# Low parts of split weights formed by accumulating transfers: four split tiles, three raw buffers

## The chip, the cores and the metric

The program runs on one core of one Trainium2 chip. The metric is the device time of one execution in microseconds (us); less is better. A core has five engines that run side by side, each through its own list of instructions in a fixed order: TensorE (PE, with its weight loads shown apart as PEld), VectorE (DVE), ScalarE (ACT), GpSimd (POOL) and SyncE (SP). They meet through semaphores alone. Transfers are issued from an engine's list and carried out by 16 DMA engines that all the issuing engines share.

## The reference

The reference is a two-layer encoder that is applied to two sequences, a prompt of 256 positions and a sample of 512, with 1024 features each. Every layer is modulated by a conditioning vector `c`: layer 0 mixes positions with a two-directional mLSTM of 4 heads, layer 1 with attention in a sliding window, and both end in a gated feed-forward network with a convolution over three positions. Cut to what matters:

```python
def trunk(x, c, ...):
    for l in range(DEPTH):                                   # DEPTH = 2
        mod = jax.nn.silu(c) @ adaln_w[l] + adaln_b[l]
        sh1, sc1, g1, sh2, sc2, g2 = split(mod, 6)
        h = rmsnorm(x, norm_g[l, 0]) * (1 + sc1) + sh1
        y = mlstm_mixer(h, ...) if l % 2 == 0 else swa_mixer(h, ...)
        x = x + g1 * y
        h = rmsnorm(x, norm_g[l, 1]) * (1 + sc2) + sh2
        x = x + g2 * conv_ffn(h, ffn_w_up[l], ffn_conv_w[l], ffn_conv_b[l], ffn_w_down[l])
    return rmsnorm(x, final_g)

def conv_ffn(h, w_up, conv_w, conv_b, w_down):
    u = conv(h @ w_up, conv_w) + conv_b                      # 2 * 2816 channels, width 3
    return (silu(u[..., :D_FF]) * u[..., D_FF:]) @ w_down
```

All data are float32, and the result must be accurate to nearly that.

## The kernel before

The 768 positions of both sequences are the columns of every activation, the 1024 features lie on 128 partitions in 8 groups. A matrix product in TensorE's fast rounded format (`R`, float32r) is too coarse alone, so both factors are **split**: a high part is the value rounded to that format, a low part is what the rounding left. Three matmuls, high by high, high by low and low by high, add up in PSUM to nearly the full product.

Weights come in units of 128 x 2048 values, and each is handled in two halves of 128 x 1024 (512 KB). `load` (L234) takes a half from device memory with one transfer from SP's queue into a tile named `raw`; there are **five** buffers of that name. `split` (L237) makes two tiles, `whi` and `wlo`, of which there are **three** buffers each: ACT writes `whi` by a copy that rounds (L222), then DVE writes `wlo` as the raw tile less `whi` (L223). There are 247 such splits. The rows of the conditioning matrix `adaln_w` also go through `raw` tiles, either multiplied by TensorE (`adaln`, L351) or by DVE (`adaln_v`, L412); each of these two generators fetches one row ahead of the one it uses. The small tiles `sb` (L384, L442) take a `raw` buffer too.

The stages, in order: the start (normalisation, first rows of `adaln_w`, gates), the four mLSTM heads with rows of `adaln_w` worked in between, the output gate, the output projection (`out_proj`, L509), the feed-forward network of layer 0 (`ffn`, L1117), then attention (`swa`), projection and feed-forward network of layer 1.

A feed-forward network takes 11 steps `p`, and a step is two calls of `pair` (L1045) and one of `down` (L1180). A `pair` loads two halves, `ra` and `rb`, adds and subtracts their quarters in place on POOL (L1053, L1055, L1056, L1079) and splits three tiles: `wa` from `ra` as it came, `wc` from `ra` after the additions, `wb` from `rb` after them (the sums of a scheme that takes 7 products of quarters where 8 would be needed). A fourth operand, `s1`, has half the size and its own tiles. Between the products ACT copies an accumulator from one PSUM bank to another (L1086, L1093), and the next product adds to the copy. `down` splits two halves (here D0 and D1). So a step has 8 splits and 6 loads. The gated product of the convolved rows is taken on POOL (L1165).

The order of instructions on each engine is not written by hand: a scheduler with a timing model of its own orders each engine's list, and a tile's buffer is given out again when the last reader of its former content is done. The lists are then fixed.

Of the kernel before, what the change touches and what calls it, by code (L numbers as in the profile page):

```python
# [10 lines left out]
F32 = mybir.dt.float32  # L11
R = mybir.dt.float32r
AF = mybir.ActivationFunctionType
ALU = mybir.AluOpType

P = 128
# [121 lines left out]
class Net:  # L138
# [88 lines left out]


    def raw(self, src):
        t = self.stg.tile([P, 1024], F32, tag="raw", name=self.nm("raw"), bufs=5)  # L230
        self.nc.sync.dma_start(t, src)
        return t

    def load(self, u, h):  # L234
        return self.raw(self.io["w"][u, :, h * 1024 : (h + 1) * 1024])

    def split(self, src):  # L237
        hi = self.stg.tile([P, 1024], R, tag="whi", name=self.nm("whi"), bufs=3)
        lo = self.stg.tile([P, 1024], R, tag="wlo", name=self.nm("wlo"), bufs=3)
        self.fp_copy_split(hi, lo, src)  # L240
        return hi, lo

    def halves(self, u):
        for h in range(2):
            yield h, self.split(self.load(u, h))

    def step(self, gen, n=1):
        for _ in range(n):
# [102 lines left out]
    def adaln(self, l, th, first=False):  # L351
        nc = self.nc
        hold = None

        def fetch(i):
            nonlocal hold
            k, h = divmod(i, 2)
            c0 = th * 2048 + h * 1024
            src = self.io["adaln_w"][l, k * P : (k + 1) * P, c0 : c0 + 1024]
            if k < 2 or not first:  # L360
                return self.raw(src)
            z = (i - 4) % 3
            if z == 0:
                hold = self.slab([P, 3, 1024])
            nc.sync.dma_start(hold[:, z], src)
            return hold[:, z]

        if not first:
            part = fetch(0)
            yield  # L370
        ps = self.ps()
        for i in range(2 * KC):
            k, h = divmod(i, 2)
            cur = fetch(i) if first else part
            if not first and i < 2 * KC - 1:
                part = fetch(i + 1)
            for g in range(2):
                r0 = 32 * (2 * h + g)
                self.mm(
                    ps[r0 : r0 + 32, :], self.silc[:, k, :], cur[:, g * 512 : (g + 1) * 512], k == 0, k == KC - 1  # L380
                )
            if i < 2 * KC - 1 and (h or not first):
                yield
        sb = self.stg.tile([P, 2, 256], F32, tag="raw", name=self.nm("sb"), bufs=5)  # L384
        sb = [sb[:, z] for z in range(2)]
        nc.vector.tensor_copy(sb[0], ps[:, :256])
        nc.scalar.copy(sb[1], ps[:, 256:])
        pt = self.ps()
        for b in range(4):
            nc.tensor.transpose(  # L390
                pt[:, b * P : (b + 1) * P], sb[b // 2][:, (b % 2) * P : (b % 2 + 1) * P], self.ident
            )
        src = pt.rearrange("p (b g s) -> p g b s", b=4, g=4)[:, :, :, 0:2]
        dst = self.mod[l][:, th * 16 : (th + 1) * 16, :].rearrange("p (g b) s -> p g b s", g=4)
        ab = self.cst(AB + 48 * l + 16 * th, 16).rearrange("p (g b) -> p g b", g=4)
        for s in range(2):
            nc.vector.tensor_tensor(dst[:, :, :, s], src[:, :, :, s], ab, ALU.add)
        i = {0: 0, 2: 1}.get(th)
        if i is not None:
            c0 = 8 if i == 0 else 32  # L400
            for s in range(2):
                nc.vector.scalar_tensor_tensor(
                    self.gain[l][i][:, :, s],
                    self.mod[l][:, c0 : c0 + 8, s],
                    1.0,
                    self.cst(NG + (2 * l + i) * 8, 8),
                    ALU.add,
                    ALU.mult,
                )
        yield  # L410

    def adaln_v(self, l, pool):  # L412

        nc = self.nc
        stt = nc.vector.scalar_tensor_tensor
        rows = [(grp, k) for grp in range(6) for k in range(KC)]
        fetch = lambda grp, k: self.raw(
            self.io["adaln_w"][l, k * P : (k + 1) * P, grp * 1024 : (grp + 1) * 1024]
        )
        raw = fetch(*rows[0])  # L420
        yield
        for grp, k in rows:
            if k == 0:
                acc = pool.tile([P, 2, 1024], F32, tag="ada", name=self.nm("ada"), bufs=1)
            row = raw
            if (grp, k) != rows[-1]:
                raw = fetch(*rows[grp * KC + k + 1])
            for s in range(2):
                w = self.silc[:, k, s : s + 1]
                if k == 0:  # L430
                    nc.vector.tensor_scalar(acc[:, s], row, w, None, ALU.mult)
                else:
                    stt(acc[:, s], row, w, acc[:, s], ALU.mult, ALU.add)
            if k < KC - 1:
                yield
                continue
            ps = self.ps()
            for s in range(2):
                for b in range(2):
                    r0 = 32 * (2 * s + b)  # L440
                    self.mm(ps[r0 : r0 + 32, :], self.ones[:, :32], acc[:, s, b * 512 : (b + 1) * 512], True, True)
            sb = self.stg.tile([P, 2, 256], F32, tag="raw", name=self.nm("sb"), bufs=5)  # L442
            sb = [sb[:, z] for z in range(2)]
            nc.vector.tensor_copy(sb[0], ps[:, :256])
            nc.scalar.copy(sb[1], ps[:, 256:])
            pt = self.ps()
            for t in range(4):
                nc.tensor.transpose(
                    pt[:, t * P : (t + 1) * P], sb[t // 2][:, (t % 2) * P : (t % 2 + 1) * P], self.ident
                )  # L450
            src = pt.rearrange("p (t g s) -> p g t s", t=4, g=4)[:, :, :, 0]
            ab = self.cst(AB + 48 * l + 8 * grp, 8).rearrange("p (b t) -> p b t", b=2)
            dst = self.mod[l][:, grp * 8 : (grp + 1) * 8, :].rearrange("p (b t) s -> p b t s", b=2)
            for s in range(2):
                nc.vector.tensor_tensor(dst[:, :, :, s], src[:, 2 * s : 2 * s + 2], ab, ALU.add)
            i = {1: 0, 4: 1}.get(grp)
            if i is not None:
                for s in range(2):
                    stt(
                        self.gain[l][i][:, :, s], self.mod[l][:, grp * 8 : (grp + 1) * 8, s], 1.0,  # L460
                        self.cst(NG + (2 * l + i) * 8, 8), ALU.add, ALU.mult,
                    )
            yield
# [45 lines left out]
    def out_proj(self, u0, act, xt, l, apply):  # L509


        def tiles():
            kept = []
            for u in range(4):
                for h, w in self.halves(u0 + u):
                    kept.append(w)
                    yield 0, 2 * u + h, w
            for c in (5, 6, 7):
                yield 1, c, kept[c]
            yield 1, 4, self.split(self.load(u0 + 2, 0))  # L520
            for u in range(2):
                for h, w in self.halves(u0 + u):
                    yield 1, 2 * u + h, w

        norms = [Norm(self, xt, half, apply) for half in HALVES]
        for i, (z, c, w) in enumerate(tiles()):
            c0, c1, _ = HALVES[z]
            o = self.ps()[:, : c1 - c0]
            self.product(o, w, act, c0, c1)
            self.tick(4.2)  # L530
            for p0, p1, q in pieces(c0, c1):
                self.resid(xt, o[:, p0 - c0 : p1 - c0], l, 16, c, (p0, p1, q))
            norms[z].square(c)
            if i % KC == KC - 1:
                self.start(HALVES[z], norms[z].stages())
# [13 lines left out]
    def mlstm(self, pool, gw, xt):  # L549
        nc, io = self.nc, self.io  # L550
# [57 lines left out]

        hsT = [self.slab([P, 4, T]) for _ in range(2)]
        for h in range(4):  # L610

            mb = self.slab([P, 4, T])
            for d in range(2):
# [10 lines left out]
            for i in range(2):  # L624
# [3 lines left out]
                t = self.slab([P, 2, 2, T], R)  # L628
# [30 lines left out]
            for q, (s0, s1) in enumerate(SEQS):  # L659
                n = (s1 - s0) // P  # L660
                for j in range(n):
# [7 lines left out]
                    w = (n + 1) * P  # L669
# [13 lines left out]
                    if q == 0:  # L683
                        t = [pool.tile([P, 640], R, tag="PT", name=self.nm("PT"), bufs=8) for _ in range(2)]
# [360 lines left out]
    def pair(self, pool, u, bank, rows, early=False, spare=False, pool_adds=True):  # L1045


        nc = self.nc
        r1, r2 = rows
        ra, rb = (self.load(u, h) for h in range(2))  # L1050
        q = [t[:, 512 * i : 512 * (i + 1)] for t in (ra, rb) for i in range(2)]
        tt = (nc.gpsimd if pool_adds else nc.vector).tensor_tensor
        tt(q[2], q[2], q[3], ALU.add)  # L1053
        wa = self.split(ra)
        tt(q[0], q[2], q[0], ALU.subtract)  # L1055
        tt(q[1], q[1], q[0], ALU.subtract)  # L1056
        if spare:
# [339 lines left out]
```

## Time and profile before

| What | Value |
|---|---|
| device time, median of 3 runs | 1947.95 us (1947.2 to 1950.5) |
| the profiled execution, device time | 1955.06 us |
| its span, first to last instruction | 1953.2 us |
| granted TensorE clock, mean over it | 0.979 |
| ACT copies to `whi` | 247, mean 1047 ns |
| DVE subtractions to `wlo` | 247, mean 1339 ns |
| loads of weights into `raw` by SP | 202, 512 KB each, 3.7 us to landing in the median |
| loads of `adaln_w` into `raw` | 84, 512 KB each, 4.3 us |
| transfers issued by POOL | none |

A row of the grouped views names the line, the engine, the operation, what is written and read, and how often; then the busy time in us and the mean length in ns, and behind the second bar the time that the engine stood idle before these instructions, with what ended it. In a timeline, a row has start, length, engine, line and operation, and in brackets the idle time before it and what released it. The lists of waits give the total in us, how often, and the longest. The 1.9 us between the span and the device time lie around the program's instructions.

### The profile page before, as it was taken

Reading aid. Unit: us, or ns where it says so; the run is one execution under the profiler, and the core shown is the slowest. Engines: PE = TensorE matmul, PEld = TensorE weight load, DVE = VectorE, ACT = ScalarE, POOL = GpSimd, SP = SyncE. Lnnn points to the kernel's source line nnn. Section 1 sums busy time; section 2 is a strip of 40 time slices with the busy share of each in tenths; the row PEclk is TensorE's granted clock in tenths of the full one; section 3 lists DMA queues with packets and bytes.
Section 4 is the critical chain, followed back from the end, with each engine's and each line's share of the span. In section 5 each row is a group of like instructions: output and inputs, shape, how many; then the busy total and the mean of one; then the engine's idle time right before and its main releaser. Section 6 shows DMA issues by size and latency. Waiting matters only on the chain. (4 is left out here: it accounts for less than half of the span.)

```text
span 1953.2 us, 28783 instructions
## 1 busy us (share of the span) xinstructions
PE 1851.3 (95%) x11122; PEld 1673.9 (86%) x11122; DVE 1390.8 (71%) x2261; ACT 895.8 (46%) x1785; POOL 555.1 (28%) x448
## 2 busy tenths in 40 slices
PE   6799999999979999999999999999799999999997
PEld 3686887888978999999999998779789999999997
DVE  4756675684577777777777765775877777777776
ACT  3343433343446444444444555774554444444442
POOL 4203011032213333333331311342123333333323
PEclk8899999999989999999999999999899999999998
DMA  9335445455212222222222221122212222222211
GB/s 341 100 100 188 150 155 198 150 157 169 76 44 76 65 66 65 65 65 65 65 66 87 98 89 49 40 85 76 65 56 65 72 69 66 72 68 65 65 33 66
DMA packets 63381, 181.32 MB, mean 93 GB/s; under 512 B 6071, under 2 KB 23735, under 8 KB 63244
## 3 DMA queue, kind: packets, MB, share of 16 engines
q1 hardware_dynamic: 63244, 179.49, 28.7%
q8 instruction: 87, 1.43, 0.3%
q14 instruction: 50, 0.41, 0.1%
HBM read 173.03 MB, written 6.43 MB: 92 GB/s over the span
## 5 line engine op out<-in xcount | busy, mean ns | idle before, releaser
L222 ACT CAST whi<-raw 128x1024 fp32r<-128x1024 f32 x247 | 258.5, 1047 | 414.0 <-PE pa L216 202.8
L223 DVE TENSOR_TENSOR wlo<-raw,whi 128x1024 fp32r<-128x1024 f32 x247 | 330.5, 1339 | 104.1 <-ACT whi L222 103.5
L216 PE MATMUL pa<-slab,whi 128*128 128x256 f32 (+1 forms) x1472 | 349.1, 335 | 3.7 <-DVE slab L507 2.6
L216 PEld LDWEIGHTS pa<-slab,whi 128*128 128x128 f32 x1472 | 253.4, 191 | 35.3 <-DVE slab L507 9.2
L507 DVE SCALAR_TENSOR_TENSOR slab<-pa,mod,slab 128x256 f32<-128x256 f32 (+1 forms) x368 | 206.9, 591 | 59.2 <-PE pa L216 59.1
L216 PE MATMUL pa<-slab,wlo 128*128 128x256 f32 (+1 forms) x736 | 234.6, 332 | 0.0
L216 PE MATMUL ps<-zh,whi 128*128 128x256 f32 (+2 forms) x688 | 230.1, 338 | 4.6 <-ACT zh L222 2.7
L216 PE MATMUL ps<-zh,wlo 128*128 128x256 f32 (+2 forms) x688 | 229.3, 337 | 2.8 <-DVE wlo L223 2.8
L216 PE MATMUL ps<-zl,whi 128*128 128x256 f32 (+2 forms) x688 | 231.0, 338 | 0.9 <-DVE zl L477 0.7
L1040 PE MATMUL ps<-zh,whi 128*128 128x384 f32 x504 | 173.7, 345 | 20.9 <-ACT ps L1093 18.2
L1041 PE MATMUL ps<-zl,whi 128*128 128x384 f32 x504 | 171.8, 341 | 4.1 <-DVE zl L223 4.1
L1042 PE MATMUL ps<-zh,wlo 128*128 128x384 f32 x504 | 171.5, 340 | 0.0
L216 PEld LDWEIGHTS pa<-slab,wlo 128*128 128x128 f32 x736 | 140.1, 191 | 12.3
L216 PEld LDWEIGHTS ps<-zh,whi 128*128 128x128 f32 x688 | 132.8, 194 | 20.2 <-ACT zh L222 3.5
L1053 POOL TENSOR_TENSOR raw<-raw 128x512 f32<-128x512 f32 x38 | 69.0, 1815 | 284.3 <-DMA raw<-in_w_dram 132.6
L216 PEld LDWEIGHTS ps<-zh,wlo 128*128 128x128 f32 x688 | 133.4, 194 | 14.1 <-DVE wlo L223 3.4
L216 PEld LDWEIGHTS ps<-zl,whi 128*128 128x128 f32 x688 | 133.4, 194 | 12.3 <-issue 1.7
L1130 DVE SCALAR_TENSOR_TENSOR slab<-slab,cstt,slab 128x771 f32<-128x771 f32 x88 | 131.5, 1496 | 1.4
L1165 POOL TENSOR_TENSOR slab<-slab 128x772 f32<-128x772 f32 x44 | 89.5, 2035 | 139.6 <-DVE slab L1130 124.8
L1055 POOL TENSOR_TENSOR raw<-raw,raw 128x512 f32<-128x512 f32 x38 | 49.1, 1291 | 266.5 <-DVE wlo L223 245.8
L1129 DVE SCALAR_TENSOR_TENSOR slab<-slab,cstt,slab 128x771 f32<-128x771 f32 x88 | 103.0, 1172 | 29.8 <-ACT slab L1127 29.8
L1040 PEld LDWEIGHTS ps<-zh,whi 128*128 128x128 f32 x504 | 96.2, 191 | 29.9 <-ACT ps L1093 24.0
(261 smaller groups left out, 4220.1 us busy)
## 6 DMA issues: line engine op xcount, KB each, us to landing
raw<-in_w_dram SPq DMA_DIRECT2D x202, 512.0 KB, 3.7
raw<-in_adaln_w_dram SPq DMA_DIRECT2D x84, 512.0 KB, 4.3
slab<-in_x_dram SPq DMA_DIRECT2D x12, 512.0 KB, 9.1
slab<-in_adaln_w_dram SPq DMA_DIRECT2D x12, 512.0 KB, 10.2
slab<-mrows SPq DMA_DIRECT2D x8, 384.0 KB, 4.8
xs<-slab SPq DMA_DIRECT2D x6, 512.0 KB, 2.9
bt<-brow SPq DMA_DIRECT2D x16, 192.0 KB, 3.2
slab<-xs SPq DMA_DIRECT2D x6, 512.0 KB, 9.3
```

The costliest lines, as they stand in the source:

```text
L216: self.nc.tensor.matmul(out, lhsT, rhs, start=start, stop=stop)
L222: nc.scalar.copy(hi, src)
L223: nc.vector.tensor_tensor(lo, src, hi.bitcast(F32), ALU.subtract)
L507: self.nc.vector.scalar_tensor_tensor(x, o, self.mod[l][:, gc + c, q : q + 1], x, ALU.mult, ALU.add)
L1040: mm(o, wh[:, k], hi[k], start=start and k == 0, stop=False, skip_group_check=True)
L1041: mm(o, wh[:, k], lo[k], start=False, stop=False, skip_group_check=True)
L1042: mm(o, wl[:, k], hi[k], start=False, stop=k == 3, skip_group_check=True)
L1053: tt(q[2], q[2], q[3], ALU.add)
L1055: tt(q[0], q[2], q[0], ALU.subtract)
L1129: stt(y[:, 1:], u[:, :-1], w(0), y[:, 1:], ALU.mult, ALU.add)
L1130: stt(y[:, :-1], u[:, 1:], w(2), y[:, :-1], ALU.mult, ALU.add)
L1165: nc.gpsimd.tensor_tensor(y, y, yrow[:, j], ALU.mult)
```

## The change

Where the flag `adds` is set, the low part is no longer a subtraction on DVE. ACT writes the rounded raw tile to `whi` as before, then a second time with its sign turned to `wlo`; then a transfer issued by POOL adds the unrounded weights to `wlo`, so that it holds raw less high. The transfer's source is the weight in device memory where the raw tile holds it unchanged (`origin` is given), else the raw tile itself. The flag is set from the second mLSTM head on and stays set. There are 4 buffers each of `whi` and `wlo` in place of 3, and 3 of `raw` in place of 5.

```diff
     def raw(self, src):
-        t = self.stg.tile([P, 1024], F32, tag="raw", name=self.nm("raw"), bufs=5)
+        t = self.stg.tile([P, 1024], F32, tag="raw", name=self.nm("raw"), bufs=3)
         self.nc.sync.dma_start(t, src)
         return t
 
     def load(self, u, h):
-        return self.raw(self.io["w"][u, :, h * 1024 : (h + 1) * 1024])
-
-    def split(self, src):
-        hi = self.stg.tile([P, 1024], R, tag="whi", name=self.nm("whi"), bufs=3)
-        lo = self.stg.tile([P, 1024], R, tag="wlo", name=self.nm("wlo"), bufs=3)
-        self.fp_copy_split(hi, lo, src)
+        return self.raw(self.weights(u, h))
+
+    def split(self, src, origin=None):
+        nc = self.nc
+        hi = self.stg.tile([P, 1024], R, tag="whi", name=self.nm("whi"), bufs=4)
+        lo = self.stg.tile([P, 1024], R, tag="wlo", name=self.nm("wlo"), bufs=4)
+        if self.adds:
+            nc.scalar.copy(hi, src)
+            nc.scalar.activation(lo, src, AF.Copy, scale=-1.0)
+            nc.gpsimd.dma_start(lo, src if origin is None else origin, accum_op=ALU.add)
+        else:
+            self.fp_copy_split(hi, lo, src)
         return hi, lo
+
+    adds = False
+
+    def weights(self, u, h):
+        return self.io["w"][u, :, h * 1024 : (h + 1) * 1024]
 
     def halves(self, u):
         for h in range(2):
-            yield h, self.split(self.load(u, h))
+            yield h, self.split(self.load(u, h), self.weights(u, h))
...
-        sb = self.stg.tile([P, 2, 256], F32, tag="raw", name=self.nm("sb"), bufs=5)
+        sb = self.stg.tile([P, 2, 256], F32, tag="raw", name=self.nm("sb"), bufs=3)
...
-            yield 1, 4, self.split(self.load(u0 + 2, 0))
+            yield 1, 4, self.split(self.load(u0 + 2, 0), self.weights(u0 + 2, 0))
...
         for h in range(4):
+            self.adds = h > 0
...
-        wa = self.split(ra)
+        wa = self.split(ra, self.weights(u, 0))
```

In the changed program 240 of the 247 splits go this way, 152 with the source in device memory and 88 with the raw tile; 7, all of the first head and the gates, stay as they were.

More of the change, by code (lines that the diff above doesn't have):

```diff
@@ L441, in adaln_v @@
                     self.mm(ps[r0 : r0 + 32, :], self.ones[:, :32], acc[:, s, b * 512 : (b + 1) * 512], True, True)
-            sb = self.stg.tile([P, 2, 256], F32, tag="raw", name=self.nm("sb"), bufs=5)
+            sb = self.stg.tile([P, 2, 256], F32, tag="raw", name=self.nm("sb"), bufs=3)
             sb = [sb[:, z] for z in range(2)]
```

## The prediction

> **What bounds the kernel now.** I read the page's busy shares first, then the waits of PE, then one step of a feed-forward network (from one `whi` copy of ACT to the same copy a step later) as a window.
>
> ```profile
> PE 1851.3 (95%) x11122; PEld 1673.9 (86%) x11122; DVE 1390.8 (71%) x2261; ACT 895.8 (46%) x1785; POOL 555.1 (28%) x448
> L222 ACT CAST whi<-raw 128x1024 fp32r<-128x1024 f32 x247 | 258.5, 1047 | 414.0 <-PE pa L216 202.8
> L223 DVE TENSOR_TENSOR wlo<-raw,whi 128x1024 fp32r<-128x1024 f32 x247 | 330.5, 1339 | 104.1 <-ACT whi L222 103.5
> 1656.69:1704.28 47.59, 46.80 (x266) 44.06 (x265) 36.42 (x40) 21.84 (x35) 16.89 (x10) 1.00 0.22 68
> PE ps L1040 <- ACT ps L1093: 18.4, 19, 3.2
> PE ps L216 <- DVE wlo L223: 2.8, 3, 1.7
> ```
>
> PE is busy 95% of the span, and in the step 46.80 of 47.59 us (the columns are window, length, then PE, PEld, DVE, ACT, POOL, granted clock, DMA share, GB/s). So PE's own work sets the time, and a step has 0.79 us to win. DVE stands at 36.42 us of 47.59: it is not the bound. The last row is the one that this change aims at, the wait for a low part: 2.8 us in the whole execution. The row above it is the largest wait of PE in the list, 18.4 us behind an ACT copy.
>
> **What is removed.** 240 subtractions of 1339 ns, 321 us of DVE's 1390.8. In the steps this lies beside PE's work and is worth nothing by itself. It is on the path only where DVE runs without a gap while PE waits for it, at the normalisation between `out_proj` and `ffn`:
>
> ```profile
> 554.46 1.22 DVE L223 TENSOR_TENSOR wlo<-raw,whi 128x1024 fp32r<-128x1024 f32 x1
> 559.89 1.22 DVE L223 TENSOR_TENSOR wlo<-raw,whi 128x1024 fp32r<-128x1024 f32 x1
> 562.69 0.69 PE L1041 MATMUL ps<-zl,s1h 128*128 128x384 f32 x1 [3.03 <-DVE zl L223]
> 558.66 0.44 PE L1040 MATMUL ps<-zh,s1h 128*128 128x384 f32 x1 [1.81 <-ACT zh L222]
> ```
>
> Two of them, 2.4 us, end before PE goes on at 562.69. But ACT makes one more pass there, and PE waits for ACT too (last row): I take 1.0 us of it back. 1.4 us a layer, **-3 us** for two layers; bounds -5 and +2.
>
> **What is added.** ACT gets 240 further passes. Their shape is that of the `whi` copy, so 1047 ns each, 251 us, which brings ACT from 46% to 59%. The transfers have no row here: nothing was issued by POOL. I build the time L from the end of ACT's second pass to a usable `wlo` out of the load's rows in two hundred microseconds of steps:
>
> ```profile
> q1 hardware_dynamic: 3731, 13.58, 21.9%
> L231 SPq DMA_DIRECT2D raw<-in_w_dram x26: 327/328/328, 1600.2 to 1798.6; - x26
> DMA to landing us min/median/max: 3.5/3.8/4.7
> L1079 POOL TENSOR_TENSOR raw<-raw,raw x8: 2004/2016/2026, 1620.7 to 1784.6; 128x512 f32<-128x512 f32 x8
> ```
>
> A load takes 3.8 us to land, and 21.9% of 200 us for 26 loads is 1.68 us of all 16 DMA engines each. The accumulating transfer moves the same bytes, but reads the old `wlo` as well. Issue on POOL: between 0.33 us (SP's issue) and 2.0 us (POOL's longest operation in a step); I take 1.2, halfway, since software work on POOL resembles the second row more than the first. Landing: between 3.5 us (the second read hidden) and twice 4.7 us (one after the other); I take 3.8 + 1.68 = 5.5, a load with a second read behind it. So L = 6.7 us, bounds 3.8 and 11.4. Where the DVE subtraction took 1.3 us, the low part comes some 6.5 us later (with the second pass of ACT).
>
> The Trainium skill, DMA: Bandwidth & Descriptors, section on the anatomy of a DMA on the SWDGE path, gives 2.0 us plus the bytes at 436 GB/s for a transfer issued by POOL, and Collectives: The Full Stack, section on the bandwidth ceiling, says that an add in a transfer costs a second read and no more; by both, L is an estimated 2.0 + 2 x 1.2 = 4.4 us, the steps' term below would be nothing, and the sum 1960 us. No run here shows either so far.
>
> **Is there cover for L?** In the instruction order of the changed program I looked, in a step in the middle of a network, for the tile with the least time between its buffer becoming free and its first use. It is the `wa` of the next step's first pair. Its buffer comes free with the last matmul of the second pair's `wc`, and between that and the third matmul of `wa`, the first that reads the low part, PE has 34 matmuls of `down` (512 and 256 columns by turns), 12 of 384 columns, and 2 with the high part:
>
> ```profile
> 1655.08 0.34 PE L1040 MATMUL ps<-bq,whi 128*128 128x384 f32 x1
> 1656.67 2.03 PE L216 MATMUL pa<-slab,whi 128*128 128x512 f32 x8
> 1658.54 0.40 PE L216 MATMUL pa<-slab,wlo 128*128 128x512 f32 x1
> 1681.00 0.40 PE L216 MATMUL pa<-slab,whi 128*128 128x256 f32 x2
> 1681.35 0.40 PE L216 MATMUL pa<-slab,whi 128*128 128x256 f32 x2
> ```
>
> From start to start, 9 of 384 columns take 1.59 us (0.177 each), 8 of 512 take 1.87 (0.234), 3 of 256 take 0.35 (0.117; one more lies between the last two rows). 17 x 0.234 + 17 x 0.117 + 14 x 0.177 = 8.4 us. ACT's two passes take 2.1, and for two handovers between engines I take 0.4: **5.9 us** are left for L. For `wc`, `wb` and D0 it is some 71 matmuls, 12.5 us, so 10.0 for L. The least cover meets L = 6.7, so PE waits 0.8 us a step. There are 10 such steps a network, 20 in all: **+16 us**; bounds 0 (L at most 5.9) and 20 x 5.5 = 110. Every step pays again, because the buffer's release is PE's own matmul and moves with it.
>
> POOL's list is one queue, and the transfer of D1, issued just ahead of that of `wa`, stands behind the addition that waits for the next `rb` to land; that load stands behind the release of a raw tile by the transfer of `wb`. Behind a late POOL transfer wait the quarter additions (L1053, L1055, L1056), so ACT's next `whi`, so the bank copies L1086 and L1093 in ACT's list, so PE. From the release of that buffer of `wb` to D1's first matmul with the low part PE has some 156 matmuls, 27.3 us; in them lie two passes of ACT (2.1), L, issue and landing of two loads (4.5), the addition (2.0) and L again: covered up to L = 9.3, so I add nothing for it.
>
> **Three raw buffers.** At the start four rows of `adaln_w` were loaded at once; now the fourth waits for the first to be used and stands in SP's list behind 11 other loads, and the ten rows from it on follow it in PE's list:
>
> ```profile
> 28.03 1.04 ACT L222 CAST whi<-raw 128x1024 fp32r<-128x1024 f32 x1 [5.00 <-DMA raw<-in_wg_dram]
> 28.85 0.71 PE L216 MATMUL pa<-kct,nr 128*128 128x128 f32 x4
> 33.19 1.05 PE L216 MATMUL ps<-slab,silc 128*32 128x512 f32 x4 [0.26 <-DMA slab<-in_adaln_w_dram]
> 36.14 15.36 POOL L491 TENSOR_SCALAR slab<-slab,gain,mod 128x256 f32<-128x256 f32 x16 [7.34 <-DVE gain L402]
> 51.47 6.73 POOL L106 TENSOR_TENSOR nt<-nt,nt 128x256 f32<-128x256 f32 x5
> 58.26 2.72 PE L216 MATMUL pa<-inv,nt 128*128 128x2 f32 x12 [5.92 <-POOL nt L106]
> ```
>
> The fourth row takes the place in SP's list of the load that landed at 28.0. Then PE has ten rows of 1.05 us from 29.2, and the last three after them: 42.9 where the last row ended at 34.2, 8.6 later. POOL's 16 modulations end at 60.2 and not at 51.5; but the new order puts three of POOL's five additions (1.35 us each) ahead of them, so PE's matmul that stood until 58.2 comes at 62.9: **+5 us**, bounds 3 and 8.6.
>
> In the heads the two fetchers of `adaln_w` hold one raw buffer each, which leaves one for the weights and the `sb` tiles:
>
> ```profile
> L216 PE MATMUL ps<-raw,silc x128: 592/593/617, 125.6 to 386.0; 128*32 128x512 f32 x128
> L433 DVE SCALAR_TENSOR_TENSOR ada<-raw,silc,ada x72: 1266/1279/2623, 111.6 to 441.2; 128x1024 f32<-128x1024 f32 x72
> L231 SPq DMA_DIRECT2D raw<-in_adaln_w_dram x69: 327/328/917, 107.8 to 424.7; - x69
> DMA to landing us min/median/max: 3.5/4.2/7.2
> 180.03 39.31 SPq L231 DMA_DIRECT2D raw<-in_adaln_w_dram x10
> ```
>
> A row holds a buffer for 4.2 us of landing and 2.5 of use on DVE: three buffers can pass one each 2.2 us, and the last row shows a demand of one each 3.9. So they suffice on average, but nothing is ahead any more. The 32 rows that PE uses (128 records, four to a row) stand in PE's fixed list, and a late one stops it. I take 0.3 us for each, **+10 us**; bounds 0 and a third of a landing each, 45.
>
> The other stages pass: `out_proj` uses a half in 4.2 us of PE, so a buffer has three times that, 12.5, for 2.1 + 6.7; the gate and attention stages are slower still.
>
> **The sum.** 1955.06 + 16 + 5 + 10 - 3 = 1983 us of device time for the profiled execution. That one stood 7.1 us over the median of the runs, so the forecast is **1976 us**, 1.4% slower.
>
> **The rivals.** 0.2%, 3.9 us, is about what a measurement of this kernel can tell from no change.
>
> *Faster by the fourth tile.* ACT's list stops at a `whi` copy whose buffer PE still reads, and the bank copy behind it is late:
>
> ```profile
> ACT whi L222 <- PE pa L216: 202.8, 39, 7.8
> 1682.14 1.05 ACT L222 CAST whi<-raw 128x1024 fp32r<-128x1024 f32 x1 [7.31 <-PE pa L216]
> 1683.10 0.47 ACT L1093 COPY ps<-ps 128x384 f32<-128x384 f32 x1
> ```
>
> That is PE's 18.4 us. With a fourth buffer ACT would not stop there; with L below 5.9 nothing is paid in the steps, and if the heads hide their rows: 1955 - 18 - 5 + 5 - 7 = 1930 us. Against it: ACT now makes two passes ahead of a bank copy, so that 1.05 us becomes 2.1 where it is ahead. It decides below L = 5.9.
>
> *Heavy.* L = 11.4, reads one after the other, over the cover of `wa` by 5.5 us a step and over that of the others by 1.4: 1955 + 110 + 28 + 15 - 7 = 2101. For it: POOL does in software what SP's row shows at 0.33. Against it: the engines are 22% busy, so there is room to overlap.
>
> *It changes nothing.* DVE is not the bound, and cost and gain cancel within 3.9 us: 1948.
>
> **How the numbers follow.** Forecast 0.48, heavy 0.20, faster 0.22, nothing 0.10. The forecast's own range, with L from 5.9 to 9 and the heads and the start at their bounds, is 1953 to 2035. Leaving out the lower third of the faster case and most of the heavy one, the range is 1934 to 2060. Slower 0.48 + 0.20 = 0.68, same 0.10, faster 0.22.
>
> **What would show it.** The transfers' landing time in the issues of POOL: 5.5 us, its issue 1.2. In the waits of PE: a new one for the transfer at L1042 in place of L1093, 0.8 us a step, steps of 48.4 us where they were 47.6; waits of `ps` for rows of `adaln_w` between 100 and 400 us; the last row of the start near 43 us. DVE near 1070 us, ACT near 1147, the engines' DMA share in the steps above twice 0.22. The forecast is wrong if the transfer lands before 4.7 us, or if POOL's issue costs several microseconds and the additions behind it come to set the step.

## The result and the profile after

| | before | after |
|---|---|---|
| device time, median | 1948.7 us (1947.2 to 1950.5) | 2198.1 us (2196.0 to 2200.9) |
| ratio, 95% interval | | 1.128 (1.126 to 1.130) |
| span of the profiled execution | 1953.2 us | 2197.2 us |

The kernel became 12.8% slower. The direction was predicted, the size (1976 us, at most 2060) was not. First the page of the changed kernel: busy times, ACT's second pass, the two kinds of DMA queue (packets, MB, share of 16 engines), and the issues with their median time to landing.

```profile
PE 1917.6 (87%) x11122; PEld 1726.7 (79%) x11122; DVE 1092.9 (50%) x2021; ACT 1111.0 (51%) x2025; POOL 703.1 (32%) x688
L245 ACT ACTIVATE wlo<-raw 128x1024 fp32r<-128x1024 f32 x240 | 254.0, 1058 | 0.0
L246 POOL DMA_DIRECT2D wlo<-in_w_dram x152 | 134.3, 884 | 765.7 <-ACT wlo L245 266.5
q0 software_dynamic: 34560, 125.84, 31.5%
raw<-in_w_dram SPq DMA_DIRECT2D x202, 512.0 KB, 5.4
wlo<-in_w_dram POOLq DMA_DIRECT2D x152, 512.0 KB, 7.9
wlo<-raw POOLq DMA_DIRECT2D x88, 512.0 KB, 5.0
```

PE fell from 95% busy to 87%, and no other engine took its place: the highest share is still PE's. So PE waits. In the median a transfer lands 7.9 us after the start of its issue when its source is device memory and 5.0 us when it is the raw tile; POOL's issue, 0.88 us, lies inside that time. The loads, 3.7 us before, now take 5.4.

Where the time went is read from the same stretches of both kernels: from the start to the first sigmoid of the output gate, from there to the first residual addition of `out_proj`, and in each feed-forward network from its first convolution to that of its eleventh step. First the kernel before, then the changed one (window, length, then PE, PEld, DVE, ACT, POOL, granted clock, DMA share, GB/s):

```profile
0.00:396.80 396.80, 357.44 (x2252) 290.81 (x2253) 247.73 (x424) 146.17 (x364) 69.94 (x70) 0.96 0.51 172
396.80:478.60 81.80, 77.87 (x470) 67.39 (x470) 49.23 (x72) 31.17 (x66) 30.03 (x24) 1.00 0.49 157
584.70:1037.00 452.30, 442.44 (x2489) 417.29 (x2488) 348.17 (x383) 212.29 (x333) 160.39 (x93) 1.00 0.22 67
1425.60:1878.60 453.00, 442.53 (x2488) 417.12 (x2487) 348.59 (x383) 212.21 (x332) 160.57 (x93) 1.00 0.22 67
```

```profile
0.00:472.20 472.20, 380.17 (x2281) 306.25 (x2282) 228.15 (x409) 167.11 (x391) 82.00 (x90) 0.91 0.56 167
472.20:570.70 98.50, 79.55 (x441) 68.26 (x440) 35.36 (x56) 39.54 (x70) 31.50 (x34) 0.90 0.65 170
677.70:1200.60 522.90, 465.38 (x2503) 437.13 (x2502) 250.97 (x307) 282.71 (x411) 215.16 (x173) 0.95 0.61 133
1608.10:2128.90 520.80, 464.30 (x2502) 437.35 (x2501) 249.65 (x307) 282.16 (x412) 215.91 (x173) 0.95 0.61 134
```

The lengths differ by 75.4 us (start and heads), 16.7 (gate), 70.6 and 67.8 (networks): 230.5 of the 244.0 us. Of the rest, attention takes 15 (from its first product to the first residual addition behind it, 237.2 to 252.1 us) and the stretch from there to the second network 7 (101.1 to 108.1); some others give a little back. In the first network PE's busy time rose by 22.9 us for the same products and its idle time, length less busy, from 9.9 to 57.5. The step of a network, the mean of the last eight in each, went from 47.6 to 55.6 us.

PE's waits in the whole execution (total, times, longest) name what it waited for:

```profile
PE ps L1056 <- DMA wlo<-in_w_dram: 71.3, 18, 5.7
PE ps L216 <- DMA wlo<-in_w_dram: 39.7, 14, 6.9
PE ps L1054 <- ACT nt L1121: 31.6, 15, 2.9
PE ps L216 <- ACT whi L244: 25.5, 11, 8.5
PE ps L216 <- DMA raw<-in_adaln_w_dram: 13.8, 6, 3.9
```

The first row is `wa`'s low part in the networks, the second the low parts of heads, gate and projections. The third, an ACT copy of an accumulator in the networks, belongs to the first: in ACT's list the copy stands behind work that waits for the same late load. In the second network these two rows are 37.3 and 16.7 us of PE's 56.5 idle. The chain of waits shows how one step gets there (start, length, what):

```profile
1855.97 8.17 DMA raw<-in_w_dram
1864.30 1.26 POOL raw L1067
1865.56 3.38 issue
1868.96 0.88 POOL wlo L246
1869.84 1.39 issue
1871.24 8.17 DMA wlo<-in_w_dram
1879.46 0.69 PE ps L1056
```

The load of `rb` for the next pair lands 8.2 us after its issue; POOL adds the quarters; then ACT makes four passes, a half-size copy and two short ones (the pieces called issue), POOL issues D1's transfer and `wa`'s, and `wa`'s takes 8.2 us. PE stood for 5.4 us of it. Why the load left so late is in the waits of SP's queue in the middle of the second network (1700 to 2100 us):

```profile
SPq L231 <- DMA wlo<-raw: 286.6, 28, 19.2
```

SP's list of loads stands behind the landing of the transfers that read a raw tile: with three raw tiles, the next pair's `ra` takes the tile of `wb`, and `rb` is behind `ra` in the list. In this step `wb`'s transfer landed at 1855.50, and the two loads left at 1855.55 and 1855.97. Such waits alone do no harm: with transfers that copy and don't add (below), SP waits as long, 207.5 us in 300 us, and the networks lose nothing. What counts is how much still follows the load.

### The profile page after: what moved, and what is told of

It reads as the page before. It is cut to its first block, busy times and chain, and to the rows that moved or that the text cites. A ratio compares the mean times of both kernels' runs of the same rounds, so it can differ in the third digit from the quotient of the medians.

```text
span 2197.2 us, 29235 instructions
## 1 busy us (share of the span) xinstructions
PE 1917.6 (87%) x11122; PEld 1726.7 (79%) x11122; DVE 1092.9 (50%) x2021; ACT 1111.0 (51%) x2025; POOL 703.1 (32%) x688
## 3 DMA queue, kind: packets, MB, share of 16 engines
q0 software_dynamic: 34560, 125.84, 31.5%
## 5 line engine op out<-in xcount | busy, mean ns | idle before, releaser
L244 ACT CAST whi<-raw 128x1024 fp32r<-128x1024 f32 x240 | 251.5, 1048 | 280.6 <-DMA raw<-in_w_dram 93.0
L246 POOL DMA_DIRECT2D wlo<-in_w_dram x152 | 134.3, 884 | 765.7 <-ACT wlo L245 266.5
L216 PE MATMUL pa<-slab,whi 128*128 128x256 f32 (+1 forms) x1472 | 359.8, 343 | 2.7 <-DVE slab L520 2.3
L216 PEld LDWEIGHTS pa<-slab,whi 128*128 128x128 f32 x1472 | 265.9, 200 | 29.6 <-DVE slab L520 3.3
L245 ACT ACTIVATE wlo<-raw 128x1024 fp32r<-128x1024 f32 x240 | 254.0, 1058 | 0.0
L1056 PE MATMUL ps<-yh,wlo 128*128 128x384 f32 x336 | 123.5, 368 | 71.3 <-DMA wlo<-in_w_dram 71.3
L1143 DVE SCALAR_TENSOR_TENSOR slab<-slab,cstt,slab 128x771 f32<-128x771 f32 x88 | 128.0, 1454 | 114.0 <-ACT slab L1141 114.0
L216 PEld LDWEIGHTS pa<-slab,wlo 128*128 128x128 f32 x736 | 147.2, 200 | 18.6 <-DMA wlo<-in_w_dram 5.3
L446 DVE SCALAR_TENSOR_TENSOR ada<-raw,silc,ada 128x1024 f32<-128x1024 f32 x84 | 111.0, 1360 | 58.3 <-DMA raw<-in_adaln_w_dram 58.3
L246 POOL DMA_DIRECT2D wlo<-raw x88 | 77.1, 876 | 183.3 <-issue 111.7
```

The costliest lines, as they stand in the source:

```text
L216: self.nc.tensor.matmul(out, lhsT, rhs, start=start, stop=stop)
L244: nc.scalar.copy(hi, src)
L245: nc.scalar.activation(lo, src, AF.Copy, scale=-1.0)
L246: nc.gpsimd.dma_start(lo, src if origin is None else origin, accum_op=ALU.add)
L1056: mm(o, wl[:, k], hi[k], start=False, stop=k == 3, skip_group_check=True)
L1143: stt(y[:, 1:], u[:, :-1], w(0), y[:, 1:], ALU.mult, ALU.add)
```

## The experiments

The table gives the median of the runs, the ratio to the kernel before (1949 to 1951 us beside each of them) with its interval, and from one profiled execution the start with the heads, the gate, and the step, as defined above.

| kernel | us | ratio | start, heads | gate | step |
|---|---|---|---|---|---|
| before | | | 396.8 | 81.8 | 47.6 |
| changed | 2198 | 1.128 (1.126 to 1.130) | 472.2 | 98.5 | 55.6 |
| buffers alone | 1957 | 1.003 (1.002 to 1.005) | 419.5 | 84.0 | 46.7 |
| adds, old buffers | 2223 | 1.138 (1.136 to 1.141) | 439.7 | 84.4 | 57.7 |
| device source only | 2100 | 1.076 (1.074 to 1.079) | 471.2 | 98.8 | 49.7 |
| raw source only | 1988 | 1.019 (1.017 to 1.021) | 416.4 | 85.5 | 47.9 |
| `wb` by DVE | 2094 | 1.073 (1.067 to 1.080) | 468.6 | 99.9 | 49.6 |
| `wa` by DVE | 2107 | 1.079 (1.076 to 1.083) | 468.7 | 96.9 | 50.1 |
| D0, D1 by DVE | 2086 | 1.069 (1.061 to 1.076) | 473.5 | 98.3 | 49.2 |
| second pass alone | 2020 | 1.035 (1.030 to 1.041) | 441.5 | 91.9 | 47.1 |
| heads by DVE | 2142 | 1.098 (1.095 to 1.101) | 419.5 | 83.9 | 56.1 |
| copy, not add | 1988 | one run | 441.8 | 92.5 | 46.6 |
| one set of 11 buffers | 1948 | 0.998 (0.997 to 1.000) | 392.7 | 83.3 | 47.3 |
| 4 raw, 4 high, 3 low | 1937 | 0.993 (0.991 to 0.994) | 407.3 | 80.7 | 47.2 |

### The parts of the change alone

Buffers alone:

```diff
-            self.adds = h > 0
+            self.adds = False
```

> The changed kernel with every low part by DVE's subtraction again, and the new buffers (3 raw, 4 and 4 split). In the changed kernel the start and the heads took 75 us more, the gate 17, the two feed-forward networks 138. Theory A (three raw buffers become too few only because a transfer that reads a raw tile, or lands late, holds it): steps at 47.6 us, no half-clock stretches in them, start and heads at 400 to 420 us, time 1950 to 1975. Theory B (three raw buffers alone starve the heads, the transfers the networks): start and heads near 470 us, time 2020 to 2045. Theory C (the fourth split tile frees ACT): a gain of up to 18 us in the networks, time 1930 to 1950.

Theory A gave the heads and the time, and C the sign in the networks: 46.7 us a step for 47.6. The three raw tiles cost 25 us in heads and gate, the fourth split tiles gave most of it back. ACT's wait for a `whi` buffer that this product of PE releases went from 202.8 us to 39.5 (waits of this kernel):

```profile
ACT whi L222 <- PE pa L216: 39.5, 21, 5.3
```

The transfers with the old buffers:

```diff
-tag="raw", ..., bufs=3    tag="whi", ..., bufs=4    tag="wlo", ..., bufs=4
+tag="raw", ..., bufs=5    tag="whi", ..., bufs=3    tag="wlo", ..., bufs=3
```

> The 240 accumulating transfers with the old buffers (5 raw, 3 and 3 split). Theory A (the loop that sets a step runs through the raw buffers: transfer of wb has landed, then the next pair's load, the addition on POOL, ACT's passes, the transfer of wa): with five raw buffers the loads start earlier, steps at 48 to 51 us instead of 56, time 2000 to 2080. Theory B (the prediction's: the landing of the transfer against the least cover between a split buffer's release and its next use): with three split tiles each cover is some 48 matmuls, 8.4 us, shorter, so steps of 60 us and more, time above 2280.

Neither hit: 57.7 us a step, nearer to B. Five raw tiles did not rescue the steps; that the three split tiles took away cover of their own is the likely reason, for PE now waits for the low parts of D0 and D1 and of the pairs' raw-source tiles as well:

```profile
PE pa L216 <- DMA wlo<-in_w_dram: 56.6, 18, 4.5
PE ps L1056 <- DMA wlo<-raw: 23.9, 23, 2.0
```

So raw tiles were not the whole cause, and theory A in that form fell. Five raw and four split tiles together were not tried.

Then the transfers by source, with the new buffers:

```diff
-        if self.adds:
+        if self.adds and origin is not None:      # device source only
+        if self.adds and origin is None:          # raw source only
```

> Only the 152 splits whose source lies in device memory go by transfer (wa, D0, D1, heads, gate, projections); wc and wb by DVE's subtraction, so no transfer holds a raw tile. New buffers. Theory A (raw tiles held by the transfers of wc and wb delay the loads): steps at 48 to 51 us, time 2030 to 2080, with start, heads and gate still 80 us too long. Theory B (the landing of wa's own transfer, some 8 us, is short of its cover of 5.9): PE keeps waiting for wa each step, steps of 50 to 54 us, time 2080 to 2150.

> The opposite: only the 88 splits whose source is the raw tile (wc and wb of every pair) go by transfer, all others by DVE's subtraction. New buffers. Theory A (raw tiles held by these transfers): steps at 51 to 55 us, start and heads as in the run with the buffers alone, time 2040 to 2110. Theory B (wa's landing): steps at 47.6 to 48.5, time within 20 us of the run with the buffers alone.

The first does not part the theories (49.7 us lies in A's range, the time in B's); the second is B's, with 31 us over the buffers alone where B allowed 20. Against the 46.7 us of the buffers alone the two add 3.0 and 1.2 us a step, but together, in the changed kernel, 8.9. That they do more than their sum is what a path in series would do that hides under PE's own 46.7 us until it is longer. A low part takes longer than DVE's by landing + ACT's pass - subtraction: 7.8 + 1.06 - 1.34 = 7.5 us from device memory, 5.2 + 1.06 - 1.34 = 4.9 from a raw tile (landings of these two kernels; the issue is inside them, so that the 8.5 and 5.8 of the next expectations count it twice). They then leave 49.7 - 7.5 = 42.2 and 47.9 - 4.9 = 43.0 us for the rest of the path, and 42.6 + 7.5 + 4.9 = 55.0 stands against the changed kernel's 55.6.

That the sum comes so near is in part luck. In the second kernel PE waits little for a transfer and mostly for an ACT copy behind the late load (second network), so its path has another end:

```profile
PE ps L1054 <- ACT ps L1107: 10.5, 9, 2.6
PE ps L1056 <- DMA wlo<-raw: 2.0, 3, 1.1
```

And the late load of `rb`, which the path holds, lands in 4.8 and 5.5 us in these two kernels but in 7.8 in the changed one (medians of the first pairs in the second network).

### Is it one path in series?

Each link alone given back to DVE:

```diff
-    wb = self.split(rb)                                # or wa, or D0 and D1
+    wb = self.split(rb, dve=True)
```

> The changed kernel, but wb (44 of the 240) by DVE's subtraction. Steps were 56 us in the changed kernel, 46.7 with no transfers, 50 with those from device memory alone, 48 with those from raw tiles alone. Theory A (one loop in series: wb's transfer has landed, load, addition, ACT, wa's transfer, PE, wb's copies; its rest is some 41.5 us, a transfer from device memory adds 8.5, one from a raw tile 5.8): the loop loses up to 5.8, less if wc's transfer, 1.9 us ahead, holds the other raw tile: steps of 50 to 53 us, time 2080 to 2140. Theory B (every transfer costs its share of busy DMA engines: 9.3 us for 8 a step): two fewer give 2.3, steps of 53.7, time 2150.

> The changed kernel, but wa (44 of the 240) by DVE's subtraction. Theory A (the loop): it loses the 8.5 us of wa's transfer, unless that of D1, issued 2.3 us ahead of it on POOL, takes its place: steps of 48 to 51 us, time 2030 to 2090. Theory B (share of busy DMA engines): steps of 53.7, time 2150, as with wb.

> The changed kernel, but D0 and D1 (44 of the 240) by DVE's subtraction. Theory A (the loop): the loop keeps wa's and wb's transfers, and loses ACT's second pass and POOL's issue for D1 ahead of wa (about 2.3 us) and D0's transfer beside the late load (1 to 2 us): steps of 51.5 to 53.5, time 2100 to 2150. Theory B (share of busy DMA engines): 53.7, 2150. Theory D (the prediction's order of covers, D1's path the only late one): steps of 47 to 49, time 2010 to 2050.

Two of eight splits a step bring 6.0, 5.4 and 6.4 of the 8.9 us, each some two thirds. Theory B, equal shares of 2.3, falls in all three. A's range of steps held `wa` (its time did not: 2107 us, at most 2090 expected), just missed `wb`, and was too cautious for D. There theory D, with D1's path alone late, came nearer (47 to 49 for 49.2 us); but `wa` is not on that path, and 5.4 us for it speak against D. PE's waits for the low part of `wa` in the second network, first in the changed kernel, then with `wb` and with D by DVE:

```profile
PE ps L1056 <- DMA wlo<-in_w_dram: 37.3, 9, 5.5
```

```profile
PE ps L1056 <- DMA wlo<-in_w_dram: 15.4, 5, 3.9
```

```profile
PE ps L1056 <- DMA wlo<-in_w_dram: 3.2, 7, 0.6
```

In neither of the last two was `wa` itself touched. With `wb` by DVE, transfers from device memory still land in 7.7 us in the second network (7.8 in the changed kernel), and what became shorter lies ahead of `wa`'s: the late load of `rb` lands in 5.2 us in place of 7.8. With D by DVE both became shorter, the late load (4.85) and `wa`'s own transfer, which there is the only one from device memory (issues of the second network):

```profile
wlo<-in_w_dram POOLq DMA_DIRECT2D x20, 512.0 KB, 5.6
```

In the changed kernel D0's transfer runs beside the late load, and D1's, issued 2.3 us ahead of `wa`'s, beside that one: this is why D weighed more than expected. The links of the path slow each other.

### ACT's pass, the add, the heads

```diff
-            nc.gpsimd.dma_start(lo, src if origin is None else origin, accum_op=ALU.add)
+            nc.vector.tensor_tensor(lo, src, hi.bitcast(F32), ALU.subtract)     # second pass alone
+            nc.gpsimd.dma_start(lo, src if origin is None else origin)          # copy, not add
```

> ACT makes its second pass for all 240 splits as in the changed kernel, but the low part is then written by DVE's subtraction and nothing is transferred by POOL. Theory A (the loop needs the transfers): steps at 46.7 to 47.7, time 1955 to 1975. Theory C (ACT's 251 us of further passes, 8.4 us a step, put off the bank copies that PE waits for): steps of 49 to 54, time 2000 to 2100.

ACT's 251 us cost 0.4 us a step, as A said, but 30 us in heads and gate. A's time, 1975 us at most, missed these; C's range holds the 2020 us, but by longer steps, which did not come. DVE's subtraction now stands behind the second pass:

```profile
DVE wlo L246 <- ACT wlo L245: 95.6, 101, 10.2
```

> The changed kernel with transfers that copy the weights into the low tile and don't add (so the low part is the whole weight, and ACT's negated pass is overwritten). Theory A (the add costs a second read, one behind the other): landing of 4 to 5 us from device memory in place of 7.9 and 3 to 4 from a raw tile in place of 5.0, steps of 48 to 51, time 2030 to 2100. Theory B (the time to landing is that of a transfer issued by POOL and of the traffic, not of the add): landing within 1 us of the changed kernel's, time above 2160.

Theory A, and more than it expected: 1988 us, and steps at the pace of the buffers alone. The instruction lists of all five engines, the bytes moved and the buffers are those of the changed kernel; only the add is gone, so that `wlo` holds the whole weight. Over six steps of the second network PE does not wait at all: 277.91 of 277.91 us busy, at a clock of 1.00. The page of this kernel (queue, then issues):

```profile
q0 software_dynamic: 34560, 125.84, 18.8%
raw<-in_w_dram SPq DMA_DIRECT2D x202, 512.0 KB, 4.3
wlo<-in_w_dram POOLq DMA_DIRECT2D x152, 512.0 KB, 5.2
wlo<-raw POOLq DMA_DIRECT2D x88, 512.0 KB, 3.0
```

A transfer keeps all 16 DMA engines busy for 18.8% of 1986.6 us / 240 = 1.56 us as a copy, and for 31.5% of 2197.2 / 240 = 2.88 us as an add, 1.85 times as long. In the medians the add takes 2.7 us more to land from device memory, 2.0 from a raw tile, and the loads that share the engines take 1.1 more. The Trainium skill, Collectives: The Full Stack, section on the bandwidth ceiling, says that a reduce-scatter, whose add needs two source reads, runs at about half the rate of an all-gather, which copies (a ratio of 1.93 measured there); the trace agrees with 1.85. By the count of links above the copies would have given 50.2 us a step (42.6, and 5.2 + 1.06 - 1.34 = 4.9 and 3.0 + 1.06 - 1.34 = 2.7), not 46.6. The late load of `rb` became shorter too, 5.3 us for 7.8, and PE's own work is a floor; the count does not explain the rest.

Last, the heads without transfers:

```diff
-            self.adds = h > 0
...
             act = self.first(pool)
+        self.adds = True
```

> The changed kernel, but the heads and the output gate keep DVE's subtraction; the transfers begin with the first output projection. Theory A (the heads lose by themselves, and nothing of it is made up later): start, heads and gate at 500 to 510 us as with the buffers alone, steps at 56 as in the changed kernel, time 2198 - 67 = 2131, between 2120 and 2145. Theory B (what the heads lose is made up where loads can run ahead): time above 2160.

A held: 2142 us, heads and gate as with the buffers alone, steps at 56.1. The heads' loss is their own and is not made up.

### Two versions without transfers

```diff
-tag="raw", ..., bufs=5    tag="whi", ..., bufs=3    tag="wlo", ..., bufs=3
+tag="stg", ..., bufs=11   tag="stg", ..., bufs=11   tag="stg", ..., bufs=11      # one set
+tag="raw", ..., bufs=4    tag="whi", ..., bufs=4    tag="wlo", ..., bufs=3       # 4, 4, 3
```

> The kernel before with DVE's subtraction, and raw, high and low tiles taken from one set of 11 buffers in place of 5, 3 and 3, so that the heads can hold more raw tiles and the networks more split ones. If the gain of the networks with four split tiles (46.7 us a step for 47.6) comes without the heads' loss of 25 us: 1925 to 1940 us. Rival: the shared set lets loads run ahead and take the buffers that the splits need: steps above 47.6, slower than 1951.

> The kernel before with DVE's subtraction and 4 raw, 4 high and 3 low buffers in place of 5, 3 and 3. The fourth high tile lets ACT go past a copy that waited for PE (18.4 us of PE's waits in the kernel before, steps 47.6), as in the run with the buffers alone (46.7); the fourth raw tile keeps most of the heads (396.8 us with five, 419.5 with three). If the high tiles alone give the gain: 1930 to 1945 us. Rival: DVE's subtraction then waits for the third low tile where ACT waited for the third high one, steps at 47.5, and the heads lose 5 to 12: 1952 to 1962.

One set of 11 brought the heads 4 us, the networks little: no difference that can be told, and neither expectation met. Four raw, four high and three low tiles are 0.7% faster than the kernel before, 1937 us. The steps are at 47.2, not 46.7: DVE waits where the fourth low tile is missing, but much less than ACT did in the kernel before (202.8 us; below, the waits of this kernel).

```profile
ACT whi L222 <- PE pa L216: 101.0, 26, 5.2
DVE wlo L223 <- PE ps L1042: 43.2, 22, 4.4
```

So what was useful in the change was at most a buffer count, and the transfers had no part in it.

## Why the prediction was wrong

| term, us of the profiled execution | predicted | measured |
|---|---|---|
| steps of both networks | +16 | +138 |
| start | +5 | 0 |
| heads and gate | +10 | +92 |
| normalisation | -3 | +3 |
| other stages | 0 | +10 |
| sum | +28 | +244 |

**What held.** PE bounds the kernel and DVE's relief is worth nothing in the steps: with 240 subtractions fewer DVE went from 71% to 50%, and where the transfers copy, the steps take 46.6 us for 46.7 with the buffers alone. ACT's pass is 1058 ns. The new wait of PE for the transfer stands where it was expected, at the low part of `wa`. L was predicted as 6.7 us within 3.8 and 11.4; from the start of the issue to the landing it is 7.9 us from device memory and 5.0 from a raw tile. With that L the rule for `wa`'s cover gives 7.9 - 5.9 = 2.0 us a step; the kernel with device-source transfers alone lost 3.0, so the rule gives the greater part of it.

**The step that failed** is the paragraph on D1's path, "covered up to L = 9.3, so I add nothing for it". It was the right path, with links too short and one of them left out; and PE met `wa`'s low part ahead of D1's, with a transfer that POOL issues 2.3 us after D1's. In the step of the chain above, from ACT's pass for `wb` to PE's start at `wa`:

```profile
1847.20 1.04 ACT L244 CAST whi<-raw 128x1024 fp32r<-128x1024 f32 x1
1848.13 1.06 ACT L245 ACTIVATE wlo<-raw 128x1024 fp32r<-128x1024 f32 x1
...
1865.60 0.62 ACT L222 CAST s1h<-raw 128x512 fp32r<-128x512 f32 x1 [7.50 <-POOL raw L1067]
```

```profile
1849.85 0.88 POOL L246 DMA_DIRECT2D wlo<-raw  x1 [1.03 <-ACT wlo L245]
1864.28 1.29 POOL L1067 TENSOR_TENSOR raw<-raw 128x512 f32<-128x512 f32 x1 [9.67 <-DMA raw<-in_w_dram]
```

It takes 1879.46 - 1847.20 = 32.3 us. The prediction had 2.1 + 6.7 + 4.5 + 2.0 + 6.7 = 22.0 for two passes, L, two loads, the addition and L, under a cover of 27.3. The load alone took 8.2 us where 4.5 had to do for two; it ran beside two other loads and D0's adding transfer, and with the adds made copies the late load of `rb` takes 5.3 us in the median for 7.8. Between the addition and `wa`'s transfer lie 5.7 us (1865.57 to 1871.24), ACT's half-size copy, which waits for the addition and stands in ACT's list ahead of both tiles' passes, then the four passes: not counted at all. `wa`'s transfer took 8.2 us for 6.7, beside D1's; `wb`'s transfer and the addition came out about as priced. And what was asked of each tile alone should have been asked of the path: it holds two transfers and a load that the transfers slow down, and it goes round once a step. With L at its measured 7.9 us the prediction's own sum gives 20 x 2.0 = 40 us for the steps, and D1's path is still covered in it (2.1 + 7.9 + 4.5 + 2.0 + 7.9 = 24.4); the other 98 us of the measured 138 lie in the links and the series that it did not have, and in PE's half clock behind each wait (last section).

**Mis-sized beside it.** In heads and gate the 10 us were for raw buffers alone; these cost 25 (buffers alone: 419.5 + 84.0 against 396.8 + 81.8), with little waiting for rows of `adaln_w` (3.2 us there, 13.8 in the changed kernel). The transfers were given no price in these stages. They cost 67 more: 31 came with ACT's second pass and the transfer as a copy, 36 with the add (534.3 against 503.5, and 570.7 against 534.3). PE's waits for low parts there went from 8.7 us with copies to 28.5 with adds. The start lost nothing: PE's last rows of `adaln_w` ended at 36.8 us, not near 43, and its matmul behind POOL's additions came at 57.8, not at 62.9 (timeline of the changed kernel). In the normalisation 3 us were lost where 3 were to be won; that was not followed further.

```profile
29.94 6.90 PE L216 MATMUL ps<-slab,silc 128*32 128x512 f32 x46
...
57.80 1.50 PE L216 MATMUL pa<-inv,nt 128*128 128x2 f32 x12 [2.27 <-POOL nt L106]
```

**The rivals.** The heavy case came nearest in number, 2101, and the 1.85 bears out its reads one after the other; but it needs an L of 11.4, and with 7.9 only `wa`'s cover is exceeded, so that the nearness is luck. The faster case rested on the fourth tile: the buffers alone do free ACT, 17 us in the networks, but the heads take it back; with four raw, four high and three low tiles it is a gain of 0.7%.

In all, by the medians, of the 247 us from 1951 (the kernel before, beside the buffers alone) to 2198 some 6 are the buffers, 31 ACT's pass and a transfer as such (the copy's 1988 less 1957), and 210 the add. The split between the last two rests on one run with copies. What is open: of the 36 us of the add in heads and gate, 20 show as PE's waits for low parts and the rest was not taken apart; and four or five raw tiles with four split ones and transfers were not tried.

## What to carry to other kernels

When an operation is replaced by one that is slower but "hidden", follow the loop that its result closes, from buffer release to buffer release, and add up all of its late links in one sum; covers that each suffice alone do not suffice in series. Count transfers as load on the same DMA engines that the loads need, and an adding transfer as nearly two. And try each part of a change by itself: here the buffer counts alone held the gain.

## What the runs showed of the hardware

How long a transfer of 512 KB takes to land hangs on what runs beside it more than on its source. In the medians an add takes 7.9 us from device memory and 5.0 from a raw tile, a copy 5.2 and 3.0. Those that overlap no other transfer whose landing the trace tells take 5.6 and 4.6 as adds (22 and 5 of them in the changed kernel) and 4.1 and 2.9 as copies (25 and 20): some 1.1 us for the source, 1.6 for the add, and the rest for the neighbours. POOL's issue of an add takes 0.88 us, of a copy 0.57 (first the changed kernel, then the copies; min, median, max in ns):

```profile
L246 POOL DMA_DIRECT2D wlo<-in_w_dram x152: 837/880/1055, 140.5 to 2150.9; - x152
```

```profile
L246 POOL DMA_DIRECT2D wlo<-in_w_dram x152: 527/570/761, 140.8 to 1941.1; - x152
```

A wait of PE costs more than its length. The windows of the changed kernel over the wait above, the next 3.41 us and the time behind them (clock in the third column from the end):

```profile
1873.54:1878.88 5.34, 0.51 (x4) 0.19 (x2) 4.97 (x7) 2.92 (x3) 5.34 (x3) 1.00 0.85 169
1878.88:1882.29 3.41, 2.83 (x9) 2.83 (x10) 1.99 (x2) 0.84 (x1) 1.04 (x2) 0.50 0.60 115
1882.29:1886.30 4.01, 4.01 (x21) 3.33 (x21) 2.68 (x4) 2.01 (x2) 0.77 (x2) 1.00 0.53 135
```

The granted clock is 0.50 for 3.4 us, from shortly before PE starts again. PE is busy for 2.83 us of them, which costs another 1.4. Over the first network PE's busy time rose by 22.9 us for the same products, at a mean clock of 0.95 where it was 1.00; that is a third of the loss there. The Trainium skill, TensorE: Matmul & The Clock Gate, section on the HAM clock gate, describes this: a PE that stood idle for a window of about 3.4 us is set to half clock until it has been busy for about 3.4 us. The trace agrees in the main: PE had stood for 4.8 us when the clock fell, and the clock was full again 2.8 us after PE's start.
